# Seven products in a written order, one 512-column retention gate, and a premultiplied end in a two-layer hybrid network

## The chip, the core and the metric

The kernel runs on one core of one Trainium2 chip. The metric is the device time of one execution in microseconds. In the text TensorE is the matrix engine (PE in the rows, its weight loads PEld), VectorE is DVE, ScalarE is ACT, GpSimd is POOL, and SyncE (SP) issues the DMAs.

## The reference

Two layers work on 128 context tokens and 512 sample tokens, 640 in all, 1024 wide. Cut to what matters here:

```python
def layer(x, cond, s0_h, s0_r, pos, p):
    sh_m, sc_m, g_m, sh_f, sc_f, g_f = ...           # from silu(cond) @ ada_w + ada_b
    h = rmsnorm(x, p["norm_mix"]) * (1.0 + sc_m) + sh_m
    y, S_a, S_b = token_mixers(h, p, s0_h, s0_r, pos)
    x = x + g_m * y
    h = rmsnorm(x, p["norm_ffn"]) * (1.0 + sc_f) + sh_f
    gate, up = jnp.split(h @ p["w_up"], 2, axis=-1)
    return x + g_f * ((jax.nn.silu(gate) * up) @ p["w_down"]), S_a, S_b

# token_mixers: nine projections of h; 4 HGRN heads and 4 retention heads, two directions each
    o_a = head_norm(o_a, ...) * jax.nn.silu(ga)      # ga, gb: 512 columns each
    o_b = head_norm(o_b, ...) * jax.nn.silu(gb)
    return jnp.concatenate([o_a, o_b], axis=-1) @ p["w_out"], S_a, S_b

# at the end, after both layers
y = x * rsqrt(mean(x * x) + EPS) * norm_final
```

## The kernel before, in words

**Precision and weights.** Every fp32 product is made of three matmuls on rounded parts: high by high, high by low, low by high. The weights come as a stream of pieces: a DMA on SyncE brings `raw`, ScalarE casts it to `wh` (L104), VectorE subtracts to get `wl` (L105). In layer 1's feed-forward part VectorE also forms sums of weight blocks (L113).

**Tiles.** The 640 tokens are 5 tiles of 128 rows (`t`), tile 0 the context. A PSUM tile from `ps` is 128 x 1024 in fp32, and there are four of them; all the stages share them.

**The stages of a layer.** First the mixer: projections, with the steps of the HGRN and retention chains put between the matmuls (names `pk`, `pu`, `po` for a chain step's matmuls, `kT` for the ScalarE copy of `pk`, `S` for the state). Then the gates: `g_unit` four times, two for HGRN and two for retention, each with 256 columns (`as_`, L824 to L826, out of `hT`); each unit waits (`finish("scan", ...)`) for the two heads that it gates, applies silu on ScalarE and a multiplication on VectorE, and leaves transposes (`pto`) in a list that the next steps empty. Then the output projection `w_out` (`cols_512` for columns 0 to 511, `as2` for the rest), then the feed-forward part.

**`cols_512`** runs 512 columns for all five tiles at once, piece of weights by piece of weights (L1200 to L1202), in three PSUM tiles with two row tiles each.

**Feed-forward in layer 1.** 22 chunks of 128 hidden units in groups of 6, 6, 5 and 5. The first two chunks are plain (L780); the other 20 go through `seven`: the product of a 2 x 2 block of weights with a 2 x 2 block of activations (halves of the inner dimension, halves of the 640 tokens) by seven block products instead of eight. Each block product is `prod`: 4 steps of the inner dimension by 3 matmuls (L713, L714, L715), 128 x 320 out. Two PSUM tiles take them: `sx` holds x0 and x1, `sy` holds y0 and y1, each pair in one tile, 512 columns apart. The order in the source is x0, x1, y0, y1, x0, x1, y1, with the readers between: a ScalarE copy of x0 (L721), VectorE subtractions (L723, L726, L728), silu of the second x0 (L731), a subtraction (L733) and silu, a subtraction of y1 (L738), and the product of the halves (L741 to L743). After each group comes its part of the down projection: twice `cols_512`, in the last group once `cols_512` and then two units of 256 columns with `as_`.

**What sets the order.** Instructions are handed to a scheduler that orders each engine's queue by its own estimates. `pin` (L351) takes an instruction out of that freedom: pinned ones keep the order in which the source gives them. Before, the matmuls of `seven` were not pinned, and matmuls of one product could be placed among those of another. Where a tile is written and read by different engines, the scheduler's framework sets semaphore waits.

**The end.** `x_add` (L1143, L1145) multiplies a projection by its gate and adds it to x; for the last down projection `sq` (L604) then sums squares on ScalarE, one slot for each column block. `final(t)` runs for each tile behind the last 256 columns: `rstd` (L612 sum of three slots, L615 mean and epsilon, both VectorE; L617 power on GpSimd), then y = x * rs * norm_final over 1024 columns on VectorE (L1315; in two halves for the last tile) and the DMA out (L1316).

Of the kernel before, what the change touches and what calls it, by code (L numbers as in the profile page):

```python
# [10 lines left out]
F32 = mybir.dt.float32  # L11
# [6 lines left out]
P = 128  # L18
# [130 lines left out]
class Net:  # L149
# [551 lines left out]
    def seven(self, act):  # L701
# [8 lines left out]
        def prod(o, w, j, h, first=True):  # L710
            hi, lo = (x[:, HK * j:HK * j + HK] for x in w)
            for k in range(HK):
                mm(o, hi[:, k], h[0][:, k], start=first and k == 0, stop=False, skip_group_check=True)  # L713
                mm(o, hi[:, k], h[1][:, k], start=False, stop=False, skip_group_check=True)  # L714
                mm(o, lo[:, k], h[0][:, k], start=False, stop=k == HK - 1, skip_group_check=True)  # L715
            if j:
                W.done()
            return 5.1e-3 * HALF
# [346 lines left out]
    def mixer(self, l, mid):  # L1065
# [28 lines left out]
        self.oT = [None] * KT  # L1094
        for u in range(4):
            self.finish("scan", (l, "hr"[u // 2], 2 * (u % 2)), (l, "hr"[u // 2], 2 * (u % 2) + 1))
            yield from self.g_unit(l, u)

    def g_unit(self, l, u):
        nc = self.nc  # L1100
        on = self.on[u]
        ot = []

        def tpose(ts):
# [9 lines left out]
            for c in range(2):  # L1114
# [7 lines left out]
                                               op0=ALU.mult, op1=ALU.subtract)  # L1122

        def evac(g, ps):
            n = len(g)
# [12 lines left out]
    def x_add(self, gates, n0, t, ps, slot):  # L1138
# [3 lines left out]
        tmp = self.adp.tile([P, 512], F32, tag="ad", name="xa")  # L1142
        nc.vector.tensor_tensor(tmp[:, :n], ps, g, op=ALU.mult)  # L1143
        xs = self.x[:, t, n0:n0 + n]
        nc.vector.tensor_tensor(xs, xs, tmp[:, :n], op=ALU.add)  # L1145
        if slot is not None:
            self.sq(t, n0, n, slot, tmp)

    def w_out(self, l):
# [4 lines left out]
        def evac(t, ps):  # L1154
            self.x_add(self.g_m, 0, t, ps, 0)
        yield from self.cols_512(src, KT, evac, self.flushT)
        if l == 0:
# [28 lines left out]

    def cols_512(self, ksrc, nk, evac, early=None):
        mm = self.nc.tensor.matmul
# [16 lines left out]
        for kk in sizes:  # L1205
            slot, = self.W.take(1)
            for t in range(NT):
                o, cost = part(t, k, slot)
                if t == NT - 1:
# [19 lines left out]
    def ffn(self, l, mid):  # L1229
# [10 lines left out]
        for ci, nch in enumerate(CH[l]):  # L1240
# [38 lines left out]
            def add(t, ps, n0, slot):  # L1279
                self.x_add(self.g_f, n0, t, ps, slot if last else None)  # L1280
            yield from self.cols_512(src, nch, lambda t, ps: add(t, ps, 0, 0))
            if not last:
                yield from self.cols_512(src, nch, lambda t, ps: add(t, ps, 512, None))
                continue
            for n in (2, 3):
# [6 lines left out]
                def evac(g, ps):  # L1292
                    t, = g
                    add(t, ps[:, :256], 256 * n, n - 1)
                    if fin:
                        if l + 1 < DEPTH:
                            self.add_norm(t, l + 1, 0)
                        else:
                            self.final(t)
                yield from self.as_(src, -(-nch // 4), [[t] for t in range(NT)], evac,  # L1300
                                    not (fin and l + 1 < DEPTH))

    def final(self, t):
        nc = self.nc
        if t == 0:
            self.nf = self.ON("nf")
            src = self.a["norm_final"]
            nc.sync.dma_start(out=self.nf[:, :DM], in_=bass.AP(src.tensor, 0, [[0, P], [1, DM]]))
        y = self.B("y")
        rs = self.rstd(t, 3)  # L1310
        dst = self.a_out(t)
        step = DM if t < NT - 1 else DM // 2
        for c in range(0, DM, step):
            sl = slice(c, c + step)
            nc.vector.scalar_tensor_tensor(y[:, sl], self.x[:, t, sl], rs, self.nf[:, sl], op0=ALU.mult, op1=ALU.mult)  # L1315
            nc.sync.dma_start(out=dst[:, sl], in_=y[:, sl])  # L1316
# [6 lines left out]
    def slots(self):  # L1323
# [23 lines left out]
        for l in range(DEPTH):  # L1347
            wi, wo, wu, wd = a["w_in"][l], a["w_out"][l], a["w_up"][l], a["w_down"][l]
            for op in ORDER:
# [3 lines left out]
                for nm in {"h": ("zf", "zb", "qa"), "r": ("qb", "kb")}.get(k, ()):  # L1353
                    ws(wi, OFF[nm] + P * j)
            for u in range(4):
                as_(wi, 0, KT, OFF["gb" if u // 2 else "ga"] + 256 * (u % 2))
            c512(wo, 0, KT, 0)
# [91 lines left out]
```

## Time and profile before

| | us |
|---|---|
| median of 3 runs (1810.15 to 1811.55) | 1810.23 |
| the profiled execution's own time | 1810.44 |
| its span | 1808.7 |
| TensorE busy | 1765.9 |
| VectorE busy | 1192.8 |
| ScalarE busy | 763.7 |
| first matmul of the seven products, from the span's start | 1382.80 |
| start of the last matmul | 1797.24 |

The span runs from the first to the last instruction of the profiled execution; the time of a run has some more around it. Busy time of TensorE counts overlapping matmuls once, and a matmul's duration is longer than the distance to the next, because they are pipelined: the price of a matmul in a row of them is read from start to start. Idle time stands in brackets behind a row, with the instruction that ended it.

### The profile page before, as it was taken

What the parts mean: (1) busy time and instruction counts of PE and PEld (TensorE: products, weight loads), DVE (VectorE), ACT (ScalarE), POOL (GpSimd) and SP (SyncE); (2) the same over time, 40 slices, a digit from 0 to 9 for tenths busy, and PEclk for the clock granted to TensorE, in tenths of its full rate; (3) what the DMA queues carried; (4) which work ended last, traced back from release to release, by engine and by line L of the source; (5) the groups of instructions that cost most, each with busy time, mean ns of one, the idle gap of its engine ahead of it and who ended that gap; (6) DMA issues with size and microseconds to landing.
All of it is one profiled execution on the core that took longest, in us unless ns stands there. A gap on an engine that the chain in (4) does not pass through costs nothing.

```text
span 1808.7 us, 29243 instructions
## 1 busy us (share of the span) xinstructions
PE 1765.9 (98%) x12019; PEld 1678.3 (93%) x12019; DVE 1192.8 (66%) x1874; ACT 763.7 (42%) x1299; POOL 49.8 (3%) x59
## 2 busy tenths in 40 slices
PE   7999999999999999999999999999999999999997
PEld 5999899998999989999899999999999989899896
DVE  6787958864854666565676656475377667666766
ACT  7685445543422212222256555455354324233242
POOL 1100000000000000000000000000000000000000
PEclk9999999999999999999999999999999999999999
DMA  9414233221533444444442121211211312223131
GB/s 335 153 51 156 76 105 111 86 70 56 163 112 117 152 155 141 144 147 134 134 129 73 51 71 54 67 53 56 70 36 47 112 47 88 82 71 100 53 105 59
DMA packets 201622, 181.96 MB, mean 101 GB/s; under 512 B 7072, under 2 KB 171136, under 8 KB 201488
## 3 DMA queue, kind: packets, MB, share of 16 engines
q1 hardware_dynamic: 196592, 177.57, 31.3%
q10 hardware_dynamic: 4640, 2.43, 0.5%
q8 instruction: 94, 1.54, 0.3%
q0 software_dynamic: 256, 0.09, 0.1%
q14 instruction: 40, 0.33, 0.1%
HBM read 175.35 MB, written 4.72 MB: 100 GB/s over the span
## 4 chain that ended last, share of the span: by engine, by line
PE 75%; DVE 11%; ACT 5%; issue 4%; DMA 3%; POOL 1%; SPq 0%; DVEq 0%; POOLq 0%; ACTq 0%
PE gw L780 24%; PE ga L1200 6%; PE ga L1201 6%; PE ga L1202 6%; PE ga L826 4%; PE ga L825 4%; PE ga L824 4%; PE pl L917 3%; PE sx L713 2%; DVE wl L105 2%; PE sx L715 2%; PE sx L714 2%; ACT wh L104 2%; PE sy L713 1%; PE sy L714 1%
## 5 line engine op out<-in xcount | busy, mean ns | idle before, releaser
L104 ACT CAST wh<-raw 128x1024 fp32r<-128x1024 f32 (+1 forms) x265 | 265.2, 1001 | 644.9 <-PE gw L780 177.1
L105 DVE TENSOR_TENSOR wl<-raw,wh 128x1024 fp32r<-128x1024 f32 (+1 forms) x265 | 306.2, 1163 | 260.4 <-ACT wh L104 257.7
L780 PE MATMUL gw<-hT,wh 128*128 128x320 f32 x2432 | 461.8, 311 | 0.0
L780 PEld LDWEIGHTS gw<-hT,wh 128*128 128x128 f32 x2432 | 380.3, 188 | 0.6
L780 PE MATMUL gw<-hT,wl 128*128 128x320 f32 x1216 | 277.3, 309 | 0.0
L780 PEld LDWEIGHTS gw<-hT,wl 128*128 128x128 f32 x1216 | 203.1, 188 | 0.0
L824 PE MATMUL ga<-wh,hT 128*128 128x256 f32 x640 | 185.5, 290 | 0.0
L825 PE MATMUL ga<-wl,hT 128*128 128x256 f32 x640 | 181.3, 283 | 0.0
L826 PE MATMUL ga<-wh,hT 128*128 128x256 f32 x640 | 181.2, 283 | 0.0
L552 DVE CUSTOM_DVE_ANT_0 junk<-adt,srow 128x1024 f32<-128x1024 f32 x128 | 156.2, 1221 | 3.2 <-DMA adt<-in_ada_t 1.3
L1200 PE MATMUL ga<-wh,act 128*128 128x512 f32 x360 | 141.8, 394 | 0.0
L1201 PE MATMUL ga<-wl,act 128*128 128x512 f32 x360 | 140.5, 390 | 0.0
L1202 PE MATMUL ga<-wh,act 128*128 128x512 f32 x360 | 138.8, 390 | 0.0
L824 PEld LDWEIGHTS ga<-wh,hT 128*128 128x128 f32 x640 | 122.4, 191 | 0.1
L825 PEld LDWEIGHTS ga<-wl,hT 128*128 128x128 f32 x640 | 122.4, 191 | 0.1
L826 PEld LDWEIGHTS ga<-wh,hT 128*128 128x128 f32 x640 | 122.3, 191 | 0.0
L1200 PEld LDWEIGHTS ga<-wh,act 128*128 128x128 f32 x360 | 67.5, 188 | 17.4 <-DVE xa L1143 4.0
L713 PE MATMUL sx<-hT,wh 128*128 128x320 f32 x240 | 77.0, 322 | 4.0 <-DVE sv L723 4.0
L1202 PEld LDWEIGHTS ga<-wh,act 128*128 128x128 f32 x360 | 67.6, 188 | 14.1
L1201 PEld LDWEIGHTS ga<-wl,act 128*128 128x128 f32 x360 | 67.6, 188 | 13.4 <-DVE wl L105 0.6
L917 PE MATMUL pl<-X 128*128 128x128 f32 x560 | 72.9, 277 | 5.2 <-ACT X L904 5.1
L1143 DVE TENSOR_TENSOR xa<-ga,gate 128x512 f32<-128x512 f32 (+1 forms) x100 | 56.2, 580 | 32.9 <-PE ga L1202 17.0
(278 smaller groups left out, 3480.8 us busy)
## 6 DMA issues: line engine op xcount, KB each, us to landing
raw<-in_w_in SPq DMA_DIRECT2D x72, 512.0 KB, 3.8
adt<-in_ada_t SPq DMA_DIRECT2D x64, 512.0 KB, 3.8
raw<-in_w_up SPq DMA_DIRECT2D x48, 512.0 KB, 3.8
raw<-in_w_up SPq DMA_DIRECT2D x80, 256.0 KB, 3.0
raw<-in_w_down SPq DMA_DIRECT2D x39, 512.0 KB, 3.7
adw<-in_ada_w SPq DMA_DIRECT2D x16, 512.0 KB, 10.5
adw<-in_ada_w SPq DMA_DIRECT2D x32, 256.0 KB, 3.0
raw<-in_w_out SPq DMA_DIRECT2D x16, 512.0 KB, 3.7
```

The lines of the kernel that those rows point to most:

```text
L104: nc.scalar.copy(hi[:, :n], raw[:, :n])
L105: nc.vector.tensor_tensor(lo[:, :n], raw[:, :n], hi[:, :n].bitcast(F32), op=ALU.subtract)
L552: r = V.tensor_tensor_reduce(out=self.junk, in0=w[:, :DM], in1=self.srow[c], scale=1.0, scalar=0.0, op0=ALU.mult, op1=ALU.add, accum_out=( ...
L713: mm(o, hi[:, k], h[0][:, k], start=first and k == 0, stop=False, skip_group_check=True)
L780: mm(o, w[:, k], self.hT[:, d, k, sl], start=k == 0 and i == 0, stop=k == KT - 1 and i == 2)
L824: mm(o, a_hi, hi[:, j], start=i == 0, stop=False)
L825: mm(o, a_hi, lo[:, j], start=False, stop=False)
L826: mm(o, a_lo, hi[:, j], start=False, stop=i == nk - 1)
L917: nc.tensor.matmul(pl[:, i * P:(i + 1) * P], X[:, TOK + i * P:TOK + (i + 1) * P], X[:, i * P:(i + 1) * P], start=True, stop=True)
L1200: mm(o, a_hi, hi[:, j], start=i == 0, stop=False)
L1201: mm(o, a_hi, lo[:, j], start=False, stop=False)
L1202: mm(o, a_lo, hi[:, j], start=False, stop=i == nk - 1)
```

## The change

1. In `seven`, the first matmul of each inner step is pinned, so the seven products are issued in the order of the source.
2. The two 256-column units of the retention gate become one unit of 512 columns, `g_pair`, on `cols_512`. All chain steps are drained before it. Its transposes wait in a list of which `cols_512` takes one at a time while more than `keep` remain; `w_out` takes the rest in the same way. The weights are laid out for it in the stream.
3. At the end x is multiplied by norm_final ahead (`scale`): columns 0 to 511 after the first block, 512 to 767 after the second. The square sums of the first two blocks are put together early (`early_ss`), the last tiles' operations are pinned in a written order, and y is x * rs on ScalarE for 768 columns and x * rs * norm_final on VectorE for 256. The last tile's output goes out in pieces of 256 and 768 columns instead of 512 and 512.

The diff, cut to its core:

```diff
@@ -710,7 +710,9 @@
             for k in range(HK):
-                mm(o, hi[:, k], h[0][:, k], start=first and k == 0, stop=False, skip_group_check=True)
+                r = mm(o, hi[:, k], h[0][:, k], start=first and k == 0, stop=False, skip_group_check=True)
+                if k == 0:
+                    self.pin(r)
                 mm(o, hi[:, k], h[1][:, k], start=False, stop=False, skip_group_check=True)
@@ -1092,14 +1094,31 @@
         self.oT = [None] * KT
-        for u in range(4):
-            self.finish("scan", (l, "hr"[u // 2], 2 * (u % 2)), (l, "hr"[u // 2], 2 * (u % 2) + 1))
+        for u in range(2):
+            self.finish("scan", (l, "h", 2 * u), (l, "h", 2 * u + 1))
             yield from self.g_unit(l, u)
-
-    def g_unit(self, l, u):
+        self.drain("scan")
+        yield from self.g_pair(l)
+
+    def g_pair(self, l):
+        nc = self.nc
+
+        def evac(t, ps):
+            sg = self.adp.tile([P, 512], F32, tag="ad", name="sg")
+            nc.scalar.activation(sg, ps, AF.Silu)
+            for h in range(2):
+                o = self.on[2 + h][:, t]
+                nc.vector.tensor_tensor(o, o, sg[:, 256 * h:256 * h + 256], op=ALU.mult)
+            if t % 2 or t == NT - 1:
+                ts = [t - 1, t] if t % 2 else [t]
+                for h in range(2):
+                    self.pendT.append(lambda h=h, ts=ts: self.tposer(l, 2 + h)(ts))
+        yield from self.cols_512(self.h_src, KT, evac, self.flushT, 2)
+
+    def tposer(self, l, u):
         nc = self.nc
         on = self.on[u]
-        ot = []
+        ot = self.oT[2 * u:2 * u + 2] if self.oT[2 * u] else []
 
@@ -1140,9 +1166,10 @@
         tmp = self.adp.tile([P, 512], F32, tag="ad", name="xa")
-        nc.vector.tensor_tensor(tmp[:, :n], ps, g, op=ALU.mult)
+        pin = self.pin if self.W.split == len(self.W.slots) and n0 == 768 else lambda r: r
+        pin(nc.vector.tensor_tensor(tmp[:, :n], ps, g, op=ALU.mult))
         xs = self.x[:, t, n0:n0 + n]
-        nc.vector.tensor_tensor(xs, xs, tmp[:, :n], op=ALU.add)
+        pin(nc.vector.tensor_tensor(xs, xs, tmp[:, :n], op=ALU.add))
         if slot is not None:
@@ -1153,7 +1180,7 @@
             self.x_add(self.g_m, 0, t, ps, 0)
-        yield from self.cols_512(src, KT, evac, self.flushT)
+        yield from self.cols_512(src, KT, evac)
         if l == 0:
@@ -1184,7 +1211,7 @@
 
-    def cols_512(self, ksrc, nk, evac, early=None):
+    def cols_512(self, ksrc, nk, evac, early=None, keep=0):
         mm = self.nc.tensor.matmul
@@ -1205,6 +1232,8 @@
             for t in range(NT):
+                if early is None and len(self.pendT) > keep and k + t > 0:
+                    self.pendT.pop(0)()
                 o, cost = part(t, k, slot)
@@ -1278,7 +1307,17 @@
                 self.x_add(self.g_f, n0, t, ps, slot if last else None)
-            yield from self.cols_512(src, nch, lambda t, ps: add(t, ps, 0, 0))
+            end = last and l + 1 == DEPTH
+            if end:
+                self.nf = self.ON("nf")
+                nf = self.a["norm_final"]
+                nc.sync.dma_start(out=self.nf[:, :DM], in_=bass.AP(nf.tensor, 0, [[0, P], [1, DM]]))
+
+            def left(t, ps):
+                add(t, ps, 0, 0)
+                if end:
+                    self.scale(t, 0, 512)
+            yield from self.cols_512(src, nch, left)
             if not last:
@@ -1292,6 +1331,9 @@
                     add(t, ps[:, :256], 256 * n, n - 1)
+                    if end and not fin:
+                        self.scale(t, 512, 768)
+                        self.early_ss(t)
                     if fin:
@@ -1300,19 +1342,37 @@
 
+    def scale(self, t, c0, c1):
+        xs = self.x[:, t, c0:c1]
+        self.nc.vector.tensor_tensor(xs, xs, self.nf[:, c0:c1], op=ALU.mult)
+
+    def early_ss(self, t):
+        V = self.nc.vector
+        ss = self.ssq[:, t, 0:1]
+        V.tensor_tensor(ss, ss, self.ssq[:, t, 1:2], op=ALU.add)
+        V.tensor_scalar(ss, ss, 1.0 / DM, EPS, op0=ALU.mult, op1=ALU.add)
+
     def final(self, t):
         nc = self.nc
-        if t == 0:
-            self.nf = self.ON("nf")
-            src = self.a["norm_final"]
-            nc.sync.dma_start(out=self.nf[:, :DM], in_=bass.AP(src.tensor, 0, [[0, P], [1, DM]]))
+        if t:
+            self.put(t - 1)
+        ms = self.sm("ms", 1)
+        self.pin(nc.vector.scalar_tensor_tensor(ms, self.ssq[:, t, 2:3], 1.0 / DM, self.ssq[:, t, 0:1], op0=ALU.mult,
+                                                op1=ALU.add))
+        self.rs = self.sm("rs", 1)
+        nc.gpsimd.tensor_tensor(self.rs, ms, self.hp[:, :1], op=ALU.pow)
+        if t == NT - 1:
+            self.put(t)
+
+    def put(self, t):
+        nc, rs = self.nc, self.rs
         y = self.B("y")
-        rs = self.rstd(t, 3)
         dst = self.a_out(t)
-        step = DM if t < NT - 1 else DM // 2
-        for c in range(0, DM, step):
-            sl = slice(c, c + step)
-            nc.vector.scalar_tensor_tensor(y[:, sl], self.x[:, t, sl], rs, self.nf[:, sl], op0=ALU.mult, op1=ALU.mult)
+        cut = 768
+        self.pin(nc.scalar.activation(y[:, :cut], self.x[:, t, :cut], AF.Copy, scale=rs))
+        self.pin(nc.vector.scalar_tensor_tensor(y[:, cut:DM], self.x[:, t, cut:], rs, self.nf[:, cut:DM], op0=ALU.mult,
+                                                op1=ALU.mult))
+        for sl in ((slice(0, DM),) if t < NT - 1 else (slice(cut, DM), slice(0, cut))):
             nc.sync.dma_start(out=dst[:, sl], in_=y[:, sl])
@@ -1352,8 +1412,9 @@
-            for u in range(4):
-                as_(wi, 0, KT, OFF["gb" if u // 2 else "ga"] + 256 * (u % 2))
+            for u in range(2):
+                as_(wi, 0, KT, OFF["ga"] + 256 * u)
+            c512(wi, 0, KT, OFF["gb"])
             c512(wo, 0, KT, 0)
```

How the order of the queues changes is shown at three places. The first is TensorE in one unit of `seven`, at the passage from product 1 (`sx<-hT`, into x0) to product 2 (`sx<-eh`, into x1); `sy` is the tile of y0 and y1. Before:

```order
L715 MATMUL sx<-hT,wl 128x320
L713 MATMUL sy<-hT,wh 128x320
L714 MATMUL sy<-hT,wh 128x320
L715 MATMUL sy<-hT,wl 128x320
L713 MATMUL sy<-hT,wh 128x320
L713 MATMUL sx<-eh,wh 128x320
L714 MATMUL sx<-eh,wh 128x320
```

After:

```order
L716 MATMUL sx<-hT,wh 128x320
L717 MATMUL sx<-hT,wl 128x320
L713 MATMUL sx<-eh,wh 128x320
L716 MATMUL sx<-eh,wh 128x320
L717 MATMUL sx<-eh,wl 128x320
```

The four matmuls of product 3 into `sy` that stood between the two products are now behind product 2; at the passages from product 3 to 4 and from 5 to 6 nothing stands between any more either.

The second is TensorE in the gates of layer 1, at one step of an HGRN chain: `pk` are transposes, `kT` is the copy of `pk` that the matmuls `pu` read, `S` is the state. Before:

```order
L943 MATMUL pk<-ident,KK 128x128 x8
...
L826 MATMUL ga<-wh,hT 128x256
L1112 MATMUL pto<-ident,on 128x128 x4
L950 MATMUL pu<-va,kT 128x128 x8
L958 MATMUL po<-va,A 128x128 x2
L960 MATMUL po<-S,QQ 128x128
```

After:

```order
L828 MATMUL ga<-wh,hT 128x256
L1131 MATMUL pto<-ident,on 128x128 x4
L945 MATMUL pk<-ident,KK 128x128 x8
L952 MATMUL pu<-va,kT 128x128 x8
L960 MATMUL po<-va,A 128x128 x2
L962 MATMUL po<-S,QQ 128x128
```

Twelve gate matmuls and the transposes `pto` stood between `pk` and `pu` (the dots leave out eleven of the twelve); now `pu` follows `pk` directly, and `pto` stands ahead of both. Up to the next matmul on the state there were 27 gate matmuls, and there are 13.

The third is VectorE behind the last matmuls, at the tiles 2 and 3 of the last block of columns (`xa`, `x`: gate and add; `tot`, `ms`: mean of squares; `y`: the output). Before:

```order
L612 TENSOR_REDUCE tot<-ssq 128x1
L1143 TENSOR_TENSOR xa<-ga,gate 128x256
L615 TENSOR_SCALAR ms<-tot 128x1
L1145 TENSOR_TENSOR x<-x,xa 128x256
L1315 SCALAR_TENSOR_TENSOR y<-x,rs,nf 128x1024
L612 TENSOR_REDUCE tot<-ssq 128x1
```

After:

```order
L1360 SCALAR_TENSOR_TENSOR ms<-ssq 128x1
L1170 TENSOR_TENSOR xa<-ga,gate 128x256
L1172 TENSOR_TENSOR x<-x,xa 128x256
L1373 SCALAR_TENSOR_TENSOR y<-x,rs,nf 128x256
L1360 SCALAR_TENSOR_TENSOR ms<-ssq 128x1
L1170 TENSOR_TENSOR xa<-ga,gate 128x256
```

The row `tot` is gone, `ms` stands for both, and the y of 1024 columns has become one of 256, behind the next tile's gate and add; ScalarE makes the other 768 columns.

## Rows read from the trace of the kernel before

In a row of the timeline the shape behind the names is that of the operands, and an xcount above 1 stands for instructions in a row.

**Rows 1.** The page's first part: busy us, share of the span, instructions.

```profile
PE 1765.9 (98%) x12019; PEld 1678.3 (93%) x12019; DVE 1192.8 (66%) x1874; ACT 763.7 (42%) x1299; POOL 49.8 (3%) x59
```

**Rows 2.** Windows; us, busy of PE, PEld, DVE, ACT, POOL, clock, DMA share, GB/s.

```profile
1382.80:1797.50 414.70, 410.41 (x2417) 373.24 (x2415) 282.92 (x410) 139.78 (x209) 1.10 (x2) 1.00 0.25 76
1504.16:1517.54 13.38, 12.96 (x86) 12.33 (x85) 10.37 (x16) 5.54 (x9) 0.00 (x0) 1.00 0.27 80
```

**Rows 3.** Timeline, TensorE; start us, us, engine line op out<-in [idle before <-releaser].

```profile
1508.66 0.30 PE L715 MATMUL sx<-hT,wl 128*128 128x320 f32 x1
...
1512.17 0.31 PE L715 MATMUL sx<-hT,wl 128*128 128x320 f32 x1
...
1272.65 0.28 PE L826 MATMUL ga<-wh,hT 128*128 128x256 f32 x1
...
1278.04 0.28 PE L826 MATMUL ga<-wh,hT 128*128 128x256 f32 x1
...
1295.21 0.39 PE L1201 MATMUL ga<-wl,oT 128*128 128x512 f32 x1
...
1304.05 0.39 PE L1201 MATMUL ga<-wl,oT 128*128 128x512 f32 x1
```

**Rows 4.** Timeline, TensorE in the same unit: a wait on VectorE.

```profile
1508.26 0.41 PE L713 MATMUL sx<-hT,wh 128*128 128x320 f32 x1 [0.42 <-DVE sv L723]
```

**Rows 5.** Timeline, product 1 to product 2, and one wait on L731 before it.

```profile
1512.83 0.19 PEld L713 LDWEIGHTS sx<-hT,wh 128*128 128x128 f32 x1 [0.17 <-ACT sgf L731]
...
1517.19 0.31 PE L715 MATMUL sx<-hT,wl 128*128 128x320 f32 x1
...
1517.54 0.43 ACT L721 COPY sv<-sx 128x320 f32<-128x320 f32 x1 [0.80 <-PE sx L715]
...
1518.01 0.19 PEld L713 LDWEIGHTS sx<-eh,wh 128*128 128x128 f32 x1 [0.19 <-ACT sv L721]
1518.02 0.42 PE L713 MATMUL sx<-eh,wh 128*128 128x320 f32 x1
...
1518.27 0.31 PE L714 MATMUL sx<-eh,wh 128*128 128x320 f32 x1
```

**Rows 6.** Timeline, VectorE's L728: behind y0 in one unit, behind L105 in another.

```profile
1391.67 0.31 PE L715 MATMUL sy<-eh,wl 128*128 128x320 f32 x1
...
1392.02 0.49 DVE L728 TENSOR_TENSOR sv<-sv,sy 128x320 f32<-128x320 f32 x1 [0.91 <-PE sy L715]
...
1510.32 1.22 DVE L105 TENSOR_TENSOR wl<-raw,wh 128x1024 fp32r<-128x1024 f32 x1
1511.49 0.49 DVE L728 TENSOR_TENSOR sv<-sv,sy 128x320 f32<-128x320 f32 x1
```

**Rows 7.** Timeline, TensorE in the gates of layer 0 and of layer 1.

```profile
343.24 1.49 PE L950 MATMUL pu<-va,kT 128*128 128x128 f32 x11 [1.50 <-ACT kT L945]
...
1235.84 0.49 PE L961 MATMUL po<-S,QQ 128*128 128x128 f32 x2 [0.32 <-DVE S L970]
```

**Rows 8.** Timeline, VectorE at the end.

```profile
1775.52 0.69 DVE L1145 TENSOR_TENSOR x<-x,xa 128x512 f32<-128x512 f32 x1
...
1790.43 0.42 DVE L1143 TENSOR_TENSOR xa<-ga,gate 128x256 f32<-128x256 f32 x1 [0.92 <-PE ga L826]
...
1791.95 0.16 DVE L612 TENSOR_REDUCE tot<-ssq 128x1 f32<-128x3 f32 x1 [0.64 <-ACT xa L604]
...
1797.69 0.41 DVE L1143 TENSOR_TENSOR xa<-ga,gate 128x256 f32<-128x256 f32 x1
...
1800.27 0.41 DVE L1143 TENSOR_TENSOR xa<-ga,gate 128x256 f32<-128x256 f32 x1
...
1803.85 1.41 DVE L1315 SCALAR_TENSOR_TENSOR y<-x,rs,nf 128x512 f32<-128x512 f32 x2 [0.73 <-POOL rs L617]
```

**Rows 9.** The page's last part, DMA issues: count, KB each, us to landing.

```profile
raw<-in_w_up SPq DMA_DIRECT2D x48, 512.0 KB, 3.8
raw<-in_w_up SPq DMA_DIRECT2D x80, 256.0 KB, 3.0
```

More of the change, by code (lines that the diff above doesn't have):

```diff
@@ L1122, in tpose, with g_unit @@
                                                op0=ALU.mult, op1=ALU.subtract)
+        return tpose
+    def g_unit(self, l, u):
+        nc = self.nc
+        on = self.on[u]
+        tpose = self.tposer(l, u)
         def evac(g, ps):
```

## The prediction

> **What bounds the kernel now.** The profiled execution took 1810.44 us, of which the span is 1808.7; the difference, 1.7 us, is taken as unchanged. The median of the runs shown, 1810.23, lies 0.2 below it, so the sum below may be read against either. The page's first part comes first: TensorE is busy for 98% of the span and VectorE for 66% [rows 1]. So time moves where TensorE stops or gets fewer columns, and at the two ends where it has nothing to do. I then read the end of layer 1 stage by stage. From the first product to the last matmul, 414.70 us, the granted clock is 1.00, that is 2.4 GHz, and VectorE is busy for 282.92, 68% [rows 2]. One whole unit of seven products takes 13.38 us, and in it VectorE works 10.37. For the price of a matmul I take runs without a wait, first start to last start: 24 steps of 320 columns in 3.51 us (0.1463 each), 45 of 256 in 5.39 (0.1198), 39 of 512 in 8.84 (0.2267) [rows 3].
>
> **The products today.** A unit is 7 products of 12 matmuls of 320 columns: 84 x 0.1463 = 12.29, so the steady unit of 13.38 loses 1.09. The stage holds 20 units, 1680 such matmuls, and for the down projection 585 of 512 and 150 of 256 columns: 245.8 + 132.6 + 18.0 = 396.4 of 414.7. Lost are 18.3, of which I put 16 down to the products (bounds: 14 and 18) and the rest to the down projection.
>
> What is lost are short waits: one on VectorE's L723, 0.42 us [rows 4], and two of 0.17 and 0.19 on ScalarE's L731 and L721 [rows 5]. The last tells the most. Product 1 ends in sx's first half with the L715 at 1517.19; ScalarE copies that half from 1517.54 for 0.43 us; and the matmul that the copy lets go at 1518.02 is the first of product 2, which goes into sx's **other** half. The wait goes by tile, not by half. Between the two, four matmuls of product 3 (into sy) fill the time, put there by the scheduler.
>
> **Part 1, the fixed order.** The pin takes that filler away: x0, x1, y0, y1, x0, x1, y1 follow one another whole. Three of six junctions then stand behind an evacuation of the same tile: product 2 behind the copy of x0 (A), product 4 behind the subtraction of y0 (B), product 6 behind the silu of product 5 (C). The junctions 2 to 3 and 4 to 5 change the tile; their readers ran during the product between. At 6 to 7 the reader, the subtraction of y1 after product 4, has had 3.5 us.
> A: from the start of the last matmul to the start of the released one 1518.02 - 1517.19 = 0.83, and the second after a wait comes 0.25 later instead of 0.146 [rows 5]. 0.83 + 0.25 - 2 x 0.146 = **0.79**.
> C: the same chain with silu in place of the copy. The nearest rows give 0.66 from matmul to matmul (1512.17 to 1512.83), with ScalarE coming straight out of a cast [rows 3, 5]; that would be 0.62. With the fixed order the casts have been done for some time when product 5 ends, as in A, so I take 0.79 and keep 0.62.
> B: VectorE starts 0.35 after the start of the last matmul (1391.67 to 1392.02) and takes 0.49 [rows 6]; with the 0.05 from end to release of A that is 0.89, and with the second step **0.85**. This holds if VectorE is free then.
> A whole unit loses 2.43. The last unit of each of the four groups has down-projection matmuls to fill B and C, as today; I give it 1.2, A and a rest. So 16 x 2.43 + 4 x 1.2 = 43.7 instead of 16: **+27.7** (with C at 0.62: +25; with the present loss at 14 or 18: 2 more or less).
> What waits behind it: with TensorE slower, casts and differences of the weights have more time per unit (10.37 of 14.7 us on VectorE), so no new wait comes from the weights.
>
> The Trainium skill, "PSUM — Partial Sum Buffer", section "PSUM bank collisions raise a hardware error", asks for a guard by bank and quadrant and lets two engines into different banks. The two halves of sx lie 512 fp32 columns apart, by that page two banks, so the chip itself would want no wait at A and C; the row at 1518.01 shows that the program sets it all the same, and the row decides.
>
> **Part 2, the retention gates.** Per layer 240 matmuls of 256 columns become 120 of 512: 28.75 - 27.20 = 1.55. The new unit evacuates each tile with one silu of 512 columns and two multiplications, and its transposes go one at a time between the tiles and into the output projection; 0.15 per layer for waits there. Twice 1.4: **-2.8** (bounds: -4, if waits of the old units behind their transposes go as well, and -0.5, if two such waits as L723's come with each).
> The Trainium skill, "TensorE: Matmul & The Clock Gate", section "Back-to-back issue gap", gives N/2.4 + 2.5 ns, so 109 ns for 256 and 216 for 512 columns; by that the saving would be 0.3 per layer. The rows stand 11 ns above it at either width, and the sum goes by the rows.
>
> **Part 3, the ripple in front of it.** All retention chains must be done before the pair, and the scheduler orders layer 1's gates anew (layer 0's chain steps stand as before). In layer 1 the eight pu now follow the eight pk directly, with the ScalarE copy of pk between them, where 12 gate matmuls stood. Layer 0 has that pattern today and shows 1.50 of idle [rows 7]; I take 1.8, as ScalarE has two casts ahead. The step of the chain on S, which today waits 0.32 behind 27 gate matmuls, gets 13: +0.5. One more pair of transposes and their reader stands closer: +0.7. Against that, pieces that waited elsewhere are gone (0.5). **+2.5** (bounds 0 and +6).
>
> **Part 4, the end.** x is multiplied by norm_final in advance: 5 operations of 512 columns at 0.69 and 5 of 256 at 0.42 [rows 8], with 10 tiny ones at 0.16 these are 7.1 us more on VectorE in the last 25 us of matmuls. Its idle time there is 4.4, in five pieces of 0.62 to 1.02, three of them like the 0.92 [rows 8], so VectorE reaches the last block some 3 us late. There it gains: per tile it has two operations of 256, a tiny one and y's 256 columns, some 1.8 us by these durations, instead of today's 2.58 with a y of 1024 columns (1797.69 to 1800.27), and catches up within four tiles: the last xa at about 1800.5, as today (1800.27). Behind it x, the square, ms, the power on GpSimd and y: y's end moves from 1805.26 (1803.85 + 1.41) to about 1803.8, since two tiny operations fall away and y is shared by ScalarE and VectorE. The last transfer is 384 KB instead of 256 KB; weights of 512 KB take 0.8 longer to land than 256 KB [rows 9], so +0.3. **-1.2** (bounds -4 and +0.5).
>
> **Sum:** 1810.44 + 27.7 - 2.8 + 2.5 - 1.2 = 1836.6; I say 1837. The 0.2% that a measurement of this kernel can tell from no change are 3.6 us.
>
> **The rivals.**
> (a) Halves wait for themselves: if the released matmul does not depend on the other half, the seven run without a break and the fixed order even removes today's waits. 1810.44 - 16 - 2.8 + 2.5 - 1.2 = 1793. For it: the halves hold different data, and by the rule of the Trainium skill's page on PSUM above two engines could work in them at once. Against it: the row at 1518.01, and the names of the program's own waits. It decides the sign: 16 x 3 + 4 x 2 = 56 junctions; the change breaks even when one costs (16 + 1.5)/56 = 0.31 us instead of 0.79. That the fixed order shows nothing, because filler stays, ends near 1810; the listing of the changed program has no filler, so little is left for it. Chances 0.06 and 0.03.
> (b) VectorE comes late to B. Today it starts L728 right out of a 1.22 us difference of the weights [rows 6], not by its input. If in the fixed order such an operation stands ahead when y0 is ready, B grows by up to 1.2 in 16 units: 10 to 19 more, 1847 to 1856. For it: 78% busy in a unit [rows 2]. Against it: the new order puts L728's successor ahead of the next difference, and the unit gets 1.3 us longer. Chance 0.11.
> (c) The forecast, 0.80: its own range by the bounds is 1837 - 3 - 2.5 - 2.8 - 2 = 1827 to 1837 + 2 + 2.3 + 3.5 + 1.7 = 1846.
> The range that leaves out no more than 2 in 10 takes in the lower part of (b): 1826 to 1850. Faster 0.07, same 0.03, slower 0.90.
>
> **What would show it.** Of the changed kernel: the unit's period, copy of x0 to copy of x0, 14.7 instead of 13.38, with three idle stretches of about 0.5 to 0.6 ahead of sx, sy, sx on TensorE, named by L723, L728 and L733. The 512-column gate at 0.2267 a step. One wait of about 1.5 on kT in layer 1's gates. The last y about 1.4 us earlier against the last matmul. Wrong is the forecast if products 1 and 2 follow without a gap (a), or if one of the three stretches is far over 0.9 (b).

## The result

The changed kernel takes 1833.38 us (median; 1832.98 to 1833.56) against 1810.19 for the kernel before: a ratio of 1.0126, 95% interval 1.0109 to 1.0144. It is slower by some 23 us. The forecast was 1837, with a range of 1826 to 1850.

The page of the changed kernel opens with the span and the busy times; before, these were a span of 1808.7 and [rows 1].

```profile
span 1831.2 us, 28760 instructions
PE 1765.6 (96%) x11779; PEld 1661.8 (91%) x11779; DVE 1193.1 (65%) x1896; ACT 770.3 (42%) x1302; POOL 49.6 (3%) x59
```

TensorE is busy for the same time as before (1765.6 against 1765.9) in a span 22.5 us longer: what came in is waiting. The windows of the changed kernel, columns as in [rows 2], show where. The first reaches from the first product to the last matmul, the second is one unit of seven products from the copy of x0 to the next copy of x0, the third goes from the first matmul of the 256-column blocks of the last down projection to the end of the span. The last row is that third stretch in the kernel before; both hold the same number of matmuls.

```profile
1380.21:1822.66 442.45, 413.94 (x2417) 372.80 (x2415) 286.63 (x431) 144.71 (x211) 1.60 (x3) 1.00 0.24 71
1511.08:1525.81 14.73, 13.11 (x84) 12.32 (x84) 10.32 (x16) 5.73 (x8) 0.00 (x0) 1.00 0.25 72
1803.11:1831.18 28.07, 19.55 (x157) 19.08 (x155) 20.40 (x58) 12.48 (x34) 2.75 (x5) 0.91 0.24 94
...
1777.95:1808.65 30.70, 19.57 (x157) 19.09 (x155) 20.06 (x44) 8.23 (x29) 2.97 (x5) 0.86 0.22 86
```

The first stage takes 442.45 instead of 414.70 and a unit 14.73 instead of 13.38 [rows 2]. The granted clock stands at 1.00 in both, the 2.4 GHz level, so the loss is not one of the clock. The timeline of TensorE has three idle stretches per unit, one at each of the junctions A, B and C. The rows show in order of time C of the unit before, then A and B of that unit (start, duration, and in brackets the idle time and its releaser):

```profile
1505.48 0.42 PE L713 MATMUL sx<-hT,wh 128*128 128x320 f32 x1 [0.53 <-ACT sgf L733]
1511.56 0.41 PE L713 MATMUL sx<-eh,wh 128*128 128x320 f32 x1 [0.52 <-ACT sv L723]
1515.92 0.41 PE L713 MATMUL sy<-eh,wh 128*128 128x320 f32 x1 [0.58 <-DVE sv L728]
```

The chain at A, in the changed kernel, is the one of [rows 5] without the filler: last matmul of product 1, ScalarE's copy, first and second matmul of product 2.

```profile
1510.73 0.31 PE L717 MATMUL sx<-hT,wl 128*128 128x320 f32 x1
...
1511.08 0.42 ACT L723 COPY sv<-sx 128x320 f32<-128x320 f32 x1 [1.24 <-PE sx L717]
...
1511.56 0.41 PE L713 MATMUL sx<-eh,wh 128*128 128x320 f32 x1 [0.52 <-ACT sv L723]
...
1511.81 0.31 PE L716 MATMUL sx<-eh,wh 128*128 128x320 f32 x1
```

From 1510.73 to 1511.56 are 0.83 us, and the next matmul follows after 0.25: the numbers of the prediction. In the whole stage there are 52 such waits: 20 at A, one in each unit, and 16 each at B and C, none of these in the last unit of a group. Taken apart by stages, each read from the first matmul of a stage to the first of the next in both traces, the 22.5 us are (the last blocks begin with their first 256-column matmul; a few of 512 columns still follow it):

| stage | before | after | difference |
|---|---|---|---|
| start to the gates of layer 0 | 320.46 | 318.11 | -2.35 |
| gates and output projection, layer 0 | 142.01 | 141.81 | -0.20 |
| feed-forward, layer 0 | 497.38 | 497.36 | 0.0 |
| mixer, gates and output projection, layer 1 | 388.04 | 388.04 | 0.0 |
| the two plain chunks, layer 1 | 34.91 | 34.89 | 0.0 |
| seven products and down projection, to the last blocks | 395.15 | 422.90 | +27.75 |
| last blocks of 256 columns to the end of the span | 30.70 | 28.07 | -2.63 |

### The profile page after: what moved, and what is told of

Same layout as the page of the kernel before. It is cut to its first block, busy times and chain, and to the rows that moved or that the text cites. A ratio compares the mean times of both kernels' runs of the same rounds, so it can differ in the third digit from the quotient of the medians.

```text
span 1831.2 us, 28760 instructions
## 1 busy us (share of the span) xinstructions
PE 1765.6 (96%) x11779; PEld 1661.8 (91%) x11779; DVE 1193.1 (65%) x1896; ACT 770.3 (42%) x1302; POOL 49.6 (3%) x59
## 4 chain that ended last, share of the span: by engine, by line
PE 80%; DVE 10%; ACT 5%; issue 3%; DMA 1%; POOL 1%; SPq 0%; POOLq 0%; ACTq 0%; DVEq 0%
PE gw L782 24%; PE ga L1227 6%; PE ga L1228 6%; PE ga L1229 6%; PE sx L713 3%; PE ga L828 3%; PE ga L827 3%; PE ga L826 3%; PE pl L919 3%; PE sx L716 3%; PE sx L717 3%; PE sy L713 2%; PE sy L717 2%; PE sy L716 2%; DVE wl L105 1%
## 5 line engine op out<-in xcount | busy, mean ns | idle before, releaser
L105 DVE TENSOR_TENSOR wl<-raw,wh 128x1024 fp32r<-128x1024 f32 (+1 forms) x265 | 307.5, 1161 | 261.7 <-ACT wh L104 261.1
L826 PE MATMUL ga<-wh,hT 128*128 128x256 f32 x480 | 139.2, 290 | 0.0
L827 PE MATMUL ga<-wl,hT 128*128 128x256 f32 x480 | 136.1, 284 | 0.0
L828 PE MATMUL ga<-wh,hT 128*128 128x256 f32 x480 | 136.0, 283 | 0.0
L826 PEld LDWEIGHTS ga<-wh,hT 128*128 128x128 f32 x480 | 91.9, 191 | 0.0
L827 PEld LDWEIGHTS ga<-wl,hT 128*128 128x128 f32 x480 | 91.8, 191 | 0.0
L828 PEld LDWEIGHTS ga<-wh,hT 128*128 128x128 f32 x480 | 91.7, 191 | 0.0
```

The costliest lines, as they stand in the source:

```text
L105: nc.vector.tensor_tensor(lo[:, :n], raw[:, :n], hi[:, :n].bitcast(F32), op=ALU.subtract)
L826: mm(o, a_hi, hi[:, j], start=i == 0, stop=False)
L827: mm(o, a_hi, lo[:, j], start=False, stop=False)
L828: mm(o, a_lo, hi[:, j], start=False, stop=i == nk - 1)
```

## The experiments

The theory was that part 1 costs 28 us, because three junctions of a unit wait for an evacuation of the other half of the same PSUM tile, and that the gates are worth nothing net. Its rivals: the loss lies in the other parts; TensorE pauses at a change of product whatever the tile; or VectorE's queue is the bound.

**Undoing part 1, and doing it alone.** The first kernel is the changed one without the pin, the second the kernel before with it.

```diff
-                r = mm(o, hi[:, k], h[0][:, k], ...)
-                if k == 0:
-                    self.pin(r)
+                mm(o, hi[:, k], h[0][:, k], ...)
```

> The changed kernel with the pin in the seven products taken out again, the rest kept. Theory (the fixed order costs 28 us by waits of a whole PSUM tile at three junctions of a unit; the copy-to-copy period of a unit was 14.73 with it and 13.38 without): the period returns to 13.4 and the time to 1833.4 - 28 = 1805, range 1802 to 1808, so some 5 us faster than before. Rival (the loss is in the other parts, gates, chains or end): within 5 us of 1833.

> The kernel before with the pin in the seven products alone. Theory: 1810.2 + 28 = 1838, range 1835 to 1842, period of a unit 14.7. Rival (the loss needs the new gates or the new end as well): 1810 to 1825.

Without the pin: 1807.73 us, ratio to the kernel before 0.9989 (0.9979 to 0.9998). With the pin alone: 1837.98, ratio 1.0155 (1.014 to 1.017). From the first product to the last blocks they take 395.5 and 422.9 us, as the kernels before (395.2) and after (422.9). The pin alone brings the loss, and the rest of the change gains some 2 us. I had expected 5 us of gain without the pin: the time lies at the upper end of the range that I gave. The 28 us had been taken off the changed kernel's time, which contains a start 2.35 us shorter; the kernel without the pin does not start as fast in its profile (last section).

**Four tiles instead of two halves of two.** The order stays pinned; x0, x1, y0 and y1 get a tile each.

```diff
-        X, Y, T = self.ps("sx"), self.ps("sy"), self.ON("sv")
-        x0, x1, y0, y1 = X[:, :HALF], X[:, 512:512 + HALF], Y[:, :HALF], Y[:, 512:512 + HALF]
+        T = self.ON("sv")
+        x0, x1, y0, y1 = (self.ps(n)[:, :HALF] for n in ("sx", "sx", "sy", "sy"))
```

> The changed kernel, same pinned order of the products, but x0, x1, y0 and y1 each in a PSUM tile of its own (all four tiles of the pool) instead of two halves of two tiles. Theory (the waits at the passages 1 to 2, 3 to 4 and 5 to 6 come only from the shared tile): they vanish, the period of a unit falls from 14.73 to 12.3 to 12.6, the time to 1833.4 - 41 = 1792, range 1787 to 1800; the last unit of each group may wait for tiles of the down projection. Rival (TensorE pauses at a change of product, or the evacuation itself holds up the matmuls): the period stays above 14 and the time above 1825. Second rival (VectorE, 10.4 us of work in a unit, becomes the bound at once): a period of 13 to 13.5, 1803 to 1812.

Measured: 1791.5 us, ratio 0.9898 (0.9884 to 0.9913), 1% faster than the kernel before. The windows of this kernel, first product to last matmul, and one unit:

```profile
1381.66:1780.55 398.89, 398.89 (x2417) 373.41 (x2415) 283.64 (x431) 145.04 (x211) 1.60 (x3) 1.00 0.26 79
1511.16:1523.48 12.32, 12.32 (x86) 12.32 (x85) 10.15 (x16) 5.74 (x8) 0.00 (x0) 1.00 0.38 109
```

TensorE does not stop once in 398.89 us; a unit of 84 matmuls takes 12.32, 0.1467 each. Its timeline at the passage from product 1 to 2, where the wait stood, runs through while ScalarE copies x0:

```profile
1510.82 0.31 PE L717 MATMUL sx<-hT,wl 128*128 128x320 f32 x1
1510.96 0.31 PE L713 MATMUL sx<-eh,wh 128*128 128x320 f32 x1
...
1511.16 0.43 ACT L723 COPY sv<-sx 128x320 f32<-128x320 f32 x1 [1.24 <-PE sx L717]
```

So the order as such costs nothing, and neither does a change of product. Against this stage without a stop (379.3 us from the first product to the last blocks) the kernel before loses 15.8 us and the changed one 43.6. Whether four tiles would be as fast without the pin was not run.

**Only sx split.** x0 and x1 get tiles of their own, y0 and y1 share one.

```diff
-        X, Y, T = self.ps("sx"), self.ps("sy"), self.ON("sv")
-        x0, x1, y0, y1 = X[:, :HALF], X[:, 512:512 + HALF], Y[:, :HALF], Y[:, 512:512 + HALF]
+        Y, T = self.ps("sy"), self.ON("sv")
+        x0, x1 = (self.ps("sx")[:, :HALF] for _ in range(2))
+        y0, y1 = Y[:, :HALF], Y[:, 512:512 + HALF]
```

> The changed kernel with x0 and x1 in tiles of their own and y0 and y1 still sharing one. Theory (each junction has its own price): the waits on the copy of x0 (passage 1 to 2) and on silu (5 to 6) go, the wait on VectorE's subtraction of y0 (3 to 4) stays at about 0.85; period 12.3 + 0.85 = 13.2, time about 1791.5 + 16 x 0.85 = 1805, range 1802 to 1808. Rival (the three waits are not additive, VectorE's takes up what the others leave): period above 13.6.

The period is 13.20 here (13.18 to 13.21 in the whole units behind the first of a group), the difference between two copies of x0 in the timeline of ScalarE, and TensorE's only idle stretch in a unit is the one at B. The rows show the two copies, the last matmul of product 3, VectorE's two operations, and the released matmul:

```profile
1507.40 0.43 ACT L724 COPY sv<-sx 128x320 f32<-128x320 f32 x1 [1.24 <-PE sx L718]
...
1510.58 0.31 PE L718 MATMUL sy<-hT,wl 128*128 128x320 f32 x1
...
1510.37 0.68 DVE L113 TENSOR_TENSOR raw<-raw 128x512 f32<-128x512 f32 x1
1510.97 0.48 DVE L729 TENSOR_TENSOR sv<-sv,sy 128x320 f32<-128x320 f32 x1
...
1511.50 0.41 PE L714 MATMUL sy<-eh,wh 128*128 128x320 f32 x1 [0.61 <-DVE sv L729]
...
1520.60 0.43 ACT L724 COPY sv<-sx 128x320 f32<-128x320 f32 x1 [1.24 <-PE sx L718]
```

13.2 - 12.32 = 0.88 is the price of B alone. Read from start to start in the changed kernel, where A and C stand beside it, B costs 0.89 + 0.25 - 2 x 0.147 = 0.85 (1515.03 to 1515.92). So the price of B stays when A and C go, and VectorE's wait does not take up what they leave. The 0.03 more are VectorE's: L729 has no idle time ahead of it, it comes straight out of L113, 0.39 behind the start of the last matmul and not 0.35. The rest of the 14.73, 1.53, is what A and C cost together.

The time, 1810.41 in one run, lies above the range that I gave (1802 to 1808). The stage shows why: from the first product to the last blocks it is 16.8 us longer than with four tiles, where I had counted 13.6. The last units of the groups do not wait at B; but in the first unit of each group VectorE is late and the wait is 0.86 to 1.16 instead of 0.61, and the down projection waits twice 0.30 on L105, which it does not with four tiles. This execution also reached the first product 2.7 us later than that of the four-tile kernel; 1.6 of them are a fall of the clock at its start (last section).

**The tile alternates.** Two shared tiles and the pin, in the order x0, y0, x1, y1, x0, y1, x1. y0 is added to the copy of x0 at once, so that its reader doesn't wait for x1.

```diff
         yield prod(x0, a, 0, self.quarter(0, 0))
         nc.scalar.copy(v2, x0)
+        yield prod(y0, b, 0, E[3])
+        V.tensor_tensor(v3, v2, y0, op=ALU.add)
         yield prod(x1, a, 1, E[2])
         V.tensor_tensor(v2, x1, v2, op=ALU.subtract)
-        b = W.get(W.used)
-        yield prod(y0, b, 0, E[3])
-        V.tensor_tensor(v3, v2, y0, op=ALU.subtract)
+        V.tensor_tensor(v3, x1, v3, op=ALU.subtract)
         yield prod(y1, b, 1, E[1])
         V.tensor_tensor(c22, v3, y1, op=ALU.subtract)
...
-        yield prod(x1, c, 1, self.quarter(1, 1))
+        yield prod(y1, d, 0, E[4], False)
+        V.tensor_tensor(c12, v2, y1, op=ALU.subtract)
+        cost = prod(x1, c, 1, self.quarter(1, 1))
```

> The changed kernel with two shared tiles and pins, but the products in an order that changes the tile each time: x0, y0, x1, y1, x0, y1, x1, with the subtraction of y0 made ahead (one VectorE operation of 0.49 more in a unit). Theory: each reader runs during the product in between, so no junction waits; period 12.3 to 12.8, time 1792, range 1787 to 1802. Rival (the pin as such, or the lost freedom of the scheduler, costs the time): above 1825. Second rival (VectorE at some 11 us in a unit is late): period about 13.3, 1803 to 1812.

Measured: 1821.3 us, ratio 1.0067 (1.0051 to 1.0084). That is neither of my numbers: the three waits are gone, but there is a new one, of 1.52, ahead of the second y1. The timeline of VectorE and of TensorE says on what:

```profile
1511.88 1.22 DVE L105 TENSOR_TENSOR wl<-raw,wh 128x1024 fp32r<-128x1024 f32 x1
1513.01 0.68 DVE L113 TENSOR_TENSOR raw<-raw 128x512 f32<-128x512 f32 x1
1513.62 1.22 DVE L105 TENSOR_TENSOR wl<-raw,wh 128x1024 fp32r<-128x1024 f32 x1
1514.75 0.48 DVE L730 TENSOR_TENSOR sv<-sv,sy 128x320 f32<-128x320 f32 x1
...
1515.29 0.42 PE L713 MATMUL sy<-eh,wh 128*128 128x320 f32 x1 [1.52 <-DVE sv L730]
```

L730 reads the first y1. It has no idle time ahead of it: VectorE came to it straight from sums and differences of the next weights, which the scheduler had put there. To tell a bad place in the queue from a VectorE that is too slow (10.66 us busy in a unit of 14.11), the next kernel moves that one instruction: it is pinned, and the weights are given back (`W.done`) behind it.

```diff
-        yield prod(y1, b, 1, E[1])
-        V.tensor_tensor(c22, v3, y1, op=ALU.subtract)
+        cost = prod(y1, b, 1, E[1], done=False)
+        self.pin(V.tensor_tensor(c22, v3, y1, op=ALU.subtract))
+        W.done()
+        yield cost
```

> The alternating order again, with one thing moved: the subtraction of y1 (L730 there) is pinned ahead of the sums and differences of the next weights on VectorE, behind which it stood. In the alternating kernel it started 1.5 us after its inputs were ready and TensorE waited 1.52 for it in each unit. Theory (that queue was the whole remaining loss, not the order of the products or the pin): period 12.3 to 12.8 instead of 14.11, time 1791 to 1800. Rival (VectorE, with 10.9 us of work in a unit, is simply too slow for two tiles): the wait moves to another of its operations and the period stays above 13.5, time above 1810.

Measured: 1792.1 us, ratio 0.9908 (0.9891 to 0.9924); the copies of x0 follow one another after 12.38 us, and TensorE does not wait once in the products. L730 now stands ahead of L105, and starts when its input is there:

```profile
1515.85 0.49 DVE L730 TENSOR_TENSOR sv<-sv,sy 128x320 f32<-128x320 f32 x1 [0.29 <-PE sy L717]
1516.25 1.22 DVE L105 TENSOR_TENSOR wl<-raw,wh 128x1024 fp32r<-128x1024 f32 x1
...
1510.57 0.43 ACT L723 COPY sv<-sx 128x320 f32<-128x320 f32 x1 [1.28 <-PE sx L717]
...
1522.95 0.43 ACT L723 COPY sv<-sx 128x320 f32<-128x320 f32 x1 [1.29 <-PE sx L717]
```

So a pinned order on two shared tiles can be as fast as four tiles, if it changes the tile at each product and the readers are not queued behind other work.

**The other parts alone.** The gate pair with its transposes, and the end, each put into the kernel before (their hunks of the diff, nothing else); and the four-tile kernel with the four gate units of before.

> The kernel before with the retention gate pair (and its late transposes) alone. Theory (from the two traces: gates and output projection together 142.0 before and 141.8 after in layer 0, mixer to output projection 388.0 and 388.0 in layer 1): the 1.55 us that the wider matmuls save per layer are used up by new waits, above all the one on kT in layer 1 (about 1.7) and one of about half a us ahead of pa in layer 0. Time within 1.5 us of the kernel before; the gates of 512 columns at 0.227 a step. Rival (the saving of 2.8 stands by itself, and the ripple came with the other parts): 2.5 to 3 us faster.

> The kernel before with the premultiplied, pinned end alone. Theory (last matmul to the end of the span 11.2 before, 8.5 after; the blocks of 256 columns 17.4 and 17.1): 2.7 to 3 us faster. Rival (my forecast of the end, in which VectorE arrives late at the last block): about 1.2 us faster, with the last xa about 3 us behind its matmul.

> Pins, new end and four tiles in the seven products, but the four gate units of 256 columns as in the kernel before. Theory (gate pair worth nothing net): within 1.5 us of the 1791.5 of the four-tile kernel with the pair. Rival (the pair is worth 2.8): 1794.

The pair alone: 1809.38 us, ratio 1.0003 (0.9993 to 1.0013), nothing. Four tiles with the old gates: 1791.57, ratio 0.9903 (0.9888 to 0.9918), against 1791.5 with the pair: nothing again. The end alone: 1806.75, ratio 0.9989 (0.998 to 0.9998); from the first matmul of the last blocks to the end of the span it takes 28.1 us (from 1777.38), where the kernel before takes 30.7, so 2.6 less in the trace, and 2.4 by the medians against the 1809.13 of the kernel before in the same series. That is a little under the 2.7 to 3 expected and twice the 1.2 of the rival.

## Why the prediction was right

The sum, 1836.6, stands 3.6 above the profiled 1832.98. Almost all of that lies at the two ends, 2.35 at the start and 1.4 at the end, and hardly any in the part that decides.

**Part 1** was forecast at +27.7 and measured at +27.75 in its stage. Each price came out as worked out: the unit 14.73 (forecast 14.7), B 0.85 (0.85), A and C together 1.5 (1.58), with C at the upper of its two bounds (0.53 of idle, 0.52 at A). Both sides of the difference held too: against the four-tile kernel, in which nothing stops, the products lose 15.8 before (forecast 16) and 43.6 after (43.7). The 56 junctions of rival (a) are 52 waits in the trace. The step that carried it was [rows 5]: an instruction that waits for an evacuation of the half that it doesn't touch. The kernels with other tiles confirm it from the other side: without the shared tile there is no wait, and the time is 1791.5, near the 1793 of the rival (a), whose condition they bring about. By the rule of the Trainium skill, "PSUM — Partial Sum Buffer", section "PSUM bank collisions raise a hardware error", two engines may work in different banks at once; the traces agree, since with separate tiles TensorE writes x1 while ScalarE reads x0, and loses nothing.

**Rival (b)**, VectorE late at B, did not come: in the changed kernel L728 starts 0.35 us after the last matmul's start, with idle time ahead of it (0.66):

```profile
1515.03 0.31 PE L717 MATMUL sy<-hT,wl 128*128 128x320 f32 x1
...
1515.38 0.49 DVE L728 TENSOR_TENSOR sv<-sv,sy 128x320 f32<-128x320 f32 x1 [0.66 <-PE sy L717]
```

Only in the very first unit that waits at B did it come straight from other work, and TensorE waited 0.94 there. The mechanism is real all the same: the alternating kernel ran into it at another operation.

**Parts 2 and 3** were forecast at -2.8 and +2.5, together -0.3, and measured at -0.2 together, but not by the steps that I gave; that the sum agrees is luck. In layer 1 the wait on kT came as forecast, the timeline of TensorE in the changed kernel gives

```profile
1228.60 0.60 PE L952 MATMUL pu<-va,kT 128*128 128x128 f32 x3 [1.50 <-ACT kT L947]
```

though at 1.50 and not the 1.8 that I took, and the two others of my sum did not come: the step on S, which I had put 0.5 longer, no longer waits its 0.32 at all, and no wait appears for the 0.7 on the transposes' side. In layer 0, where I had expected none, the wait ahead of `pa` grew from 0.53 to 1.05, here before and after:

```profile
356.11 1.13 PE L1021 MATMUL pa<-QR 128*128 128x128 f32 x8 [0.53 <-DVE on L985]
...
354.29 0.91 PE L1023 MATMUL pa<-QR 128*128 128x128 f32 x6 [1.05 <-DVE on L987]
```

The kernel with the gate pair alone has the same two waits (1.50 and 1.08), so they come with the pair. The pitch held: in layer 1's pair 87 steps take 19.74 us, 0.227 each. But the saving was smaller than the 1.55 per layer that the pitches say, since after each group of transposes the second matmul comes about 0.09 late, in the unit of 512 columns and in the output projection behind it, as here in layer 1, 0.31 behind the first:

```profile
1257.93 0.38 PE L1131 MATMUL pto<-ident,on 128*128 128x128 f32 x2
1258.07 0.48 PE L1227 MATMUL ga<-wh,hT 128*128 128x512 f32 x1
1258.38 0.39 PE L1228 MATMUL ga<-wl,hT 128*128 128x512 f32 x1
```

These make 1.7 us of such excess over the pitch among the 512-column matmuls of layer 0, where the kernel before has 0.5 there and 0.4 more among those of 256. My 0.15 per layer for this was too small. The waits named make +1.7 in both layers (0.53, and 1.50 less 0.32) instead of +2.5, which leaves -1.9 for the gates instead of -2.8: two errors that cancel.

**Part 4** was forecast at -1.2 and measured at -2.6. VectorE was late at the last block as forecast, but by 1.6 us and not by 3 (the first xa of that block starts 5.2 ahead of the last matmul's start, where before it was 6.8, 1790.43 in [rows 8]), and it caught up faster. The step that failed is the price of the added operations: I had added up their durations, which come to 7.0 in the trace as forecast, but the next operation of VectorE starts before the one ahead has ended, and from start to start they take 5.6 (0.60 for a duration of 0.69, 0.33 for 0.42, 0.07 for many of the tiny ones). The timeline of VectorE in the changed kernel, at two operations of 512 columns (0.60 apart), at the first xa of the last block and at the last tiles:

```profile
1806.04 0.68 DVE L1170 TENSOR_TENSOR xa<-ga,gate 128x512 f32<-128x512 f32 x1
1806.64 0.68 DVE L1347 TENSOR_TENSOR x<-x,nf 128x512 f32<-128x512 f32 x1
...
1817.16 0.42 DVE L1170 TENSOR_TENSOR xa<-ga,gate 128x256 f32<-128x256 f32 x1
...
1821.93 0.42 DVE L1170 TENSOR_TENSOR xa<-ga,gate 128x256 f32<-128x256 f32 x1
1822.38 0.42 DVE L1172 TENSOR_TENSOR x<-x,xa 128x256 f32<-128x256 f32 x1
...
1822.75 0.48 DVE L1373 SCALAR_TENSOR_TENSOR y<-x,rs,nf 128x256 f32<-128x256 f32 x1
...
1823.44 0.16 DVE L1360 SCALAR_TENSOR_TENSOR ms<-ssq 128x1 f32<-128x1 f32 x1 [0.21 <-ACT xa L604]
1823.52 0.42 DVE L1170 TENSOR_TENSOR xa<-ga,gate 128x256 f32<-128x256 f32 x1
```

A tile takes 1.59 us, not 1.8, with 0.21 of idle in it. So the last xa starts 1.1 us after the start of the last matmul (1822.38), where before it was 3.0 (1800.27 and 1797.24), and the forecast had kept it at 3.3. The end of the last y, counted from the last matmul, comes 3.6 us earlier, where I had said 1.4. Against that, from there to the end of the span, behind the larger last transfer, it is 4.3 us instead of 3.4: 0.9 more and not 0.3.

The lower end of the forecast's own range, 1827, leaves out the bound of part 2 (-4); with it that end is 1825.5. The stated range hardly changes by that.

**Not forecast at all** were 2.35 us at the start, which do not come from the change: up to the gates of layer 0 TensorE, VectorE and ScalarE have the same instructions in the same order in both traces. Where they lie is told in the last section. Without them the kernel would stand at 1835.3 in the profiled run, against the 1837 of the sum.

## What to carry to other kernels

When the order of matmuls is written by hand, look at every passage where the next one writes a tile that the previous one's reader is still emptying: in this program dependencies go by tile, and a half that nobody reads is no refuge. Give each accumulator its own tile, or change tiles at every step, before fixing an order; the price of a passage could be read here beforehand from a wait of the same kind, start of the last matmul to start of the released one, plus the delay of the second. And where the order of one engine is fixed, look at the queue of the engine that frees its tiles: one small reader behind three larger jobs took back 1.7 of the 2.4 us per unit that the new order had removed. And add up the work of an engine by the distance from start to start, not by durations, as for matmuls: that was the largest miss in part 4.

## What the runs showed of the hardware

The kernel before does not start alike in all executions. In its profiled one the granted clock of TensorE fell soon after the first matmuls of layer 0; the windows (columns as in [rows 2]) of the kernel before and of the changed one from 40 to 46 us are

```profile
40.00:42.00 2.00, 2.00 (x15) 1.99 (x16) 1.81 (x5) 2.00 (x3) 0.20 (x1) 1.00 1.01 377
42.00:44.00 2.00, 2.00 (x8) 2.00 (x7) 2.00 (x5) 2.00 (x5) 0.00 (x0) 0.54 1.08 369
44.00:46.00 2.00, 2.00 (x9) 2.00 (x9) 1.96 (x6) 1.75 (x5) 0.00 (x0) 0.61 1.17 317
...
40.00:42.00 2.00, 2.00 (x13) 1.99 (x13) 1.91 (x6) 2.00 (x4) 0.00 (x0) 1.00 1.05 372
42.00:44.00 2.00, 2.00 (x13) 2.00 (x12) 1.83 (x4) 2.00 (x5) 0.00 (x0) 1.00 1.09 344
44.00:46.00 2.00, 2.00 (x14) 2.00 (x13) 1.91 (x6) 1.74 (x5) 0.00 (x0) 1.00 1.19 323
```

At about half, the 1.2 GHz level, matmuls stand 0.32 apart instead of 0.17. Of the eleven profiles three show such a fall here: the kernel before, the one without the pin, and the one with only sx split. From the first of these matmuls (40.81 in the kernel before) to the first into `ga` (63.62) these three take 22.8 us and the other eight 21.2: the fall costs 1.6 of the 2.35 us. The rest stands ahead of it: that first matmul comes 0.7 later (40.10 in the changed kernel).

In the kernel before, and in the one without the pin, TensorE had idled 0.49 and 0.22 us for a ScalarE copy some 3 and 2 us ahead of the fall; but the four-tile kernel with the old gates idled 0.42 at the same place and kept its clock, and the one with only sx split fell without such an idle time. The alternating kernel has a fall of the same size among its products (1715.7 to 1719.1, granted clock 0.50), right behind a wait of 1.74, while equal waits in two other units left its clock at 1.00. So what decides stays open. Runs of one kernel lie two or three microseconds apart, as much as the end or the gates are worth, and the mean granted clock of a run goes with it: of the ten runs with the gate pair alone, the four at 0.997 took 1810.28 to 1811.39 us, the six at 0.998 took 1808.25 to 1809.49. For parts of that size the stages of the traces say more than the medians.
